# A Strassen-style down projection: weight sums made ahead of time in the attention, deeper look-ahead, and a later last statistic

## The chip, the cores and the metric

The kernel runs on one NeuronCore of a Trainium2 chip. A core has five engines that run their own instruction streams and meet at semaphores: TensorE (PE in the profile; PEld are its weight loads), VectorE (DVE), ScalarE (ACT), GpSimd (POOL) and SyncE (SP), which in this kernel only issues DMA transfers, all of them, from one queue, in order. The metric is device time in microseconds, the median of several runs.

## The reference, cut to what matters

One decoder layer on 1024 tokens of width 1024, in float32, with three sub-layers, each normalised before and after and added to the residual stream:

```python
for l in range(DEPTH):
    h = rmsnorm(x, g_mix_pre[l])
    ...                                    # S5 state space + chunked gMLP mixers
    x = x + rmsnorm(mix, g_mix_post[l])
    h = rmsnorm(x, g_x_pre[l])
    mem_n = rmsnorm(mem, g_mem[l])
    xa = memory_cross_attention(h, mem_n, w_q[l], w_k[l], w_v[l], w_o[l])   # 4 heads, 256 memory tokens
    x = x + rmsnorm(xa, g_x_post[l])
    h = rmsnorm(x, g_ffn_pre[l])
    f = conv_ffn(h, w_up[l], conv_w[l], conv_b[l], w_down[l])
    x = x + rmsnorm(f, g_ffn_post[l])

def conv_ffn(h, w_up, conv_w, conv_b, w_down):
    a = causal_depthwise_conv(h @ w_up, conv_w, conv_b)
    val, gate = jnp.split(a, 2, axis=-1)
    return (val * jax.nn.gelu(gate)) @ w_down        # w_down: 2816 x 1024
```

## The kernel before, in words

**Layout.** Activations are held transposed, channels on the 128 partitions and tokens along the free dimension, in tiles of 128x512, so each tensor has two token halves, h = 0 and 1. Every float32 matmul is made of three passes: an operand is split into a rounded part (an ACT cast) and a rest (a DVE or POOL subtraction), and high x high, high x low and low x high are summed in PSUM (`mm3`, the matmuls of L232). The splits of streamed weights are L130 and L133, those of other operands L251 and L252 (`split`).

**Stages.** `mixers`, `attention`, `ffn` and `down` follow each other in one program. A scheduler places the instructions of all stages on the engines by its own simulated times; each engine then runs its list strictly in order. Only where `self.pinned` is set does `pin` keep the written order. Tiles come from pools with a fixed number of buffers per tag ("b" 32, "m" 16, "w" 13, "raw" 4 and so on), and a transfer into a tile waits on SP until the buffer is free.

**Attention.** For each token half h, `attention` makes the queries of four heads (`q_block`), the scores and the softmax (`scores`), the transposes (`turn`), the weighted values (`weigh`) and the output projection (`proj`, "o2"). Beside it run generators: `post[h]` finishes the mixers' sub-layer (normalise at L722 on DVE, add the residual at L723 on POOL, sum the squares at L709), and `post2[h]` does the same for the attention. The q blocks of a half need `post[h]` to be done.

**Down projection.** `w_down` and the gated activations (kept in DRAM as `fd`) are taken as 2x2 blocks with 11 slices of 128 channels in each half of the contraction. Seven block products replace eight, after Strassen and Winograd:

- phase 0: W11·a and W12·b
- phase 1: S2·T2 and S1·T1
- phase 2: S3·T3 and S4·d
- phase 3: W22·T4

with S1 = W21 + W22, S2 = S1 − W11, S3 = W11 − W21, S4 = W12 − S2 on the weights, and T1 = c − a, T2 = d − T1, T3 = d − c, T4 = b − T2 on the activations, slice by slice. A phase has 11 steps k. In phases 0 to 2 a step is 24 matmuls of 128x512, 12 into the four "acc" banks (A) and 12 into three "sx" banks and the "st" bank (B), so three matmuls into `st` end each step. `d_prep(n)` walks ahead of PE: `d_load` issues a step's transfers, `d_sums` makes the sums (L1374; all on POOL but T1, which is on DVE), `d_split` makes four splits per step (L251 on ACT, L252 on DVE). Loads run 2 steps ahead of the splits, sums 1 step. At the ends of phases the banks are copied or added out (`ready`, L1445 to L1454).

**Tail.** Phase 3 is done by token quarters of 256. While the first quarter of token half 1 is multiplied, `first_half` squares and sums the finished half 0 (adds on DVE), and `finish` scales it (L765) and adds the residual `rs` loaded from DRAM (L766), both on DVE; there are 4 `rs` buffers for 8 residual tiles. Then the order is pinned; in the pass over the second quarter, the statistics of the first quarter are taken at `TAIL_R` (`rms`: matmuls at L277, then 11 small DVE instructions, L280 and L260 to L269) and broadcast at `TAIL_B` (`bcast`, L304), where a pair (b, k) names the block and the slice after which they stand.

Of the kernel before, what the change touches and what calls it, by code (L numbers as in the profile page):

```python
# [43 lines left out]
Q_STATS = 3  # L44
TAIL_R = (0, 7)
TAIL_B = (1, 4)
T_FROM = 11
T_RATE = 1
FETCH = 2
D_LOAD = 2  # L50
D_FIRST = {"S3": 1, "22": 2}
# [99 lines left out]
class Builder:  # L151
# [602 lines left out]
    def finish(self, m, acc, h, x2d):  # L754
# [8 lines left out]
        for i in range(KT):  # L763
            x = m[i]
            v.scalar_tensor_tensor(x, x, self.gain["g_ffn_post"][:, i:i + 1], bc, ALU.mult, ALU.mult)  # L765
            v.tensor_tensor(x, x, res[i], ALU.add)  # L766
            yield
            nc.sync.dma_start(self.out[P * i:P * i + P, HALF * h:HALF * h + HALF], x)
# [33 lines left out]
    def prepare(self, cp, dp):  # L802
# [71 lines left out]
        self.x2d = halves("x2d", 8)  # L874
        self.fd = halves("fd", NP)
        self.p1d = [dram(f"p1d{i}", [P, HALF]) for i in range(NP)]
        self.v0d = [dram(f"v0d{i}", [P, HALF]) for i in range(NP)]
# [168 lines left out]
    def attention(self):  # L1046
# [109 lines left out]
        sq2 = [None, None]  # L1156
        self.post2 = [None, None]
        for h in range(2):
            heads = lambda k, hh: oT[hh][k]
            for i in range(6):  # L1160
                if i == 5:
                    for b in range(EARLY):
                        begin(heads, "o2", b, h, range(6))
                if i == 1:
                    self.drain(post[h])
                if 1 <= i <= 4:
                    scores(h, i - 1)
                for j in range(2):
                    if i < 4:
                        q_block(h, i, j)  # L1170
                    if i >= 2:
                        turn(i - 2) if j == 0 else weigh(h, i - 2)
# [160 lines left out]


    def d_load(self, n):
        nc = self.nc
# [9 lines left out]
        if ph == 0:  # L1346
            get("11", w(0, 0), "b")
            get("12", w(0, 1), "raw")
            get("a", x(0, 1), "t" if n < 2 else "f")
            get("b", x(1, 1), "t" if n < 2 else "fr")  # L1350
        elif ph == 1:
            if k < 2:
                get("a", x(0, 1), "f")
            get("21", w(1, 0), "f")
            get("22", w(1, 1), "b")
            get("c", x(0, 0), "f")
            get("d", x(1, 0), "f")
        elif ph == 2:
            get("11", w(0, 0), "b")
            get("21", w(1, 0), "f")  # L1360
            get("12", w(0, 1), "raw")
            get("c", x(0, 0), "f")
# [5 lines left out]
    def d_sums(self, n):  # L1368
        v, g = self.nc.vector, self.nc.gpsimd
        ph, k = divmod(n, 11)  # L1370
        s = self.ds[k]

        def sub(key, to, x, y, e=g, op=ALU.subtract):
            e.tensor_tensor(s[to], s[x], s[y], op)  # L1374
            s[key] = s[to]

        if ph == 1:
            sub("S1", "22", "21", "22", g, ALU.add)
            sub("S2", "11", "S1", "11")
            sub("T1", "c", "c", "a", v)  # L1380
            sub("T2", "a", "d", "T1")
        elif ph == 2:
            sub("S3", "21", "11", "21")
            sub("S4", "S2", "12", "S2")
            sub("T3", "c", "d", "c")
# [3 lines left out]
    def d_split(self, n):  # L1389
# [3 lines left out]
        for i, key in enumerate(names):  # L1393
# [4 lines left out]
            hl = self.dp[n, i] = self.pair(tag)  # L1398
            self.split(*hl, s.pop(key) if key not in ("S2", "T2", "11", "a", "d") else s[key])

    def d_prep(self, n):

        while self.n_prep < min(n, 44):
            i = self.n_prep
            while self.n_load <= min(i + D_LOAD, self.d_last):
                self.d_load(self.n_load)
                self.n_load += 1
            while self.n_sums <= min(i + 1, 43):
                self.d_sums(self.n_sums)
                self.n_sums += 1  # L1410
# [9 lines left out]
    def down(self):  # L1420
# [54 lines left out]
        def first_half():  # L1475
            for b in range(8):
                self.sumsq(m[b], sq[0], b == 0, v)
                if b % 2:
                    yield
# [25 lines left out]
        self.drain(job)  # L1505
        self.pinned = True
        st = {}
        for b in range(4):
            for k in range(11):
                one(k, b, quarters[1])  # L1510
# [91 lines left out]
```

## Time and profile before

| | us |
|---|---|
| median of 3 runs | 1379.97 (1378.66 to 1382.13) |
| the profiled execution, whole | 1384.13 |
| its span, first to last instruction | 1382.4 |

In that execution the mean granted TensorE clock was 0.958. Times inside the trace count from the span's start. "Busy" of an engine leaves out waiting; "idle before, releaser" in a row is the time that the engine stood still just before those instructions, and what it waited for. Matmuls are pipelined, so the mean of one matmul record (some 390 ns) is longer than the spacing of two. In a row of windows the columns are the stretch, its length, the busy time of PE, PEld, DVE, ACT and POOL (with the number of instructions), the granted clock, the share of the DMA engines, and GB/s. The down projection begins near 1113 us; its phase 3 begins at 1319.75 us.

### The profile page before, as it was taken

To read this page: it belongs to the slowest core of one execution; us is meant where nothing else is said; L and a number is where in the kernel's file an instruction comes from. 1 tells how busy PE (TensorE), PEld (TensorE's weight loads), DVE (VectorE), ACT (ScalarE), POOL (GpSimd) and SP (SyncE) were. 2 spreads that over 40 slices of the span, in tenths; PEclk is the share of its full clock that TensorE was granted. 3 is DMA by queue.
4 is the path that set the end of the run, shared out by engine and by line. 5 is a ranking of instruction groups with operands and counts; after the bars stand their busy time and mean duration, and the time that the engine had idled before them with its cause. 6 is when DMAs were issued, how large, how long until landed. Compare 5 with 4: busy or idle time off the path is not lost. (4 is left out here: it accounts for less than half of the span.)

```text
span 1382.4 us, 19079 instructions
## 1 busy us (share of the span) xinstructions
PE 1281.1 (93%) x6352; PEld 1084.1 (78%) x6352; DVE 1064.7 (77%) x1645; ACT 627.3 (45%) x1172; POOL 662.5 (48%) x506
## 2 busy tenths in 40 slices
PE   9799998779998999989999999999999999896984
PEld 8689897678886887778887788888888887775883
DVE  7968799875375647785578969789988889997675
ACT  7223331246453545445445645555555553336340
POOL 1576346734254005420455477665664128995302
PEclk9899999889998999999999999999999999998996
DMA  9644326356344214452376674545554297556224
GB/s 314 191 140 133 89 82 174 84 154 182 99 123 152 64 53 142 134 157 62 114 244 208 210 257 156 165 146 162 165 156 145 77 336 243 178 171 214 77 70 152
DMA packets 139572, 213.38 MB, mean 154 GB/s; under 512 B 32464, under 2 KB 41808, under 8 KB 139472
## 3 DMA queue, kind: packets, MB, share of 16 engines
q1 hardware_dynamic: 139472, 212.15, 49.0%
q8 instruction: 50, 0.82, 0.2%
q14 instruction: 50, 0.41, 0.1%
HBM read 165.58 MB, written 42.32 MB: 150 GB/s over the span
## 5 line engine op out<-in xcount | busy, mean ns | idle before, releaser
L232 PE MATMUL acc<-b,w 128*128 128x512 f32 x2412 | 593.9, 399 | 26.1 <-ACT m L1450 11.0
L232 PEld LDWEIGHTS acc<-b,w 128*128 128x128 f32 x2412 | 461.2, 193 | 126.9 <-ACT m L1450 11.4
L133 DVE TENSOR_TENSOR w<-raw,w 128x512 fp32r<-128x512 f32 x206 | 194.3, 950 | 102.1 <-PE acc L232 72.8
L232 PE MATMUL sx<-b,w 128*128 128x512 f32 x921 | 223.7, 392 | 2.0 <-ACT T L1270 1.9
L232 PEld LDWEIGHTS sx<-b,w 128*128 128x128 f32 x921 | 174.3, 190 | 39.5 <-ACT T L1270 2.3
L130 ACT CAST w<-raw 128x512 fp32r<-128x512 f32 x228 | 141.4, 622 | 121.6 <-PE acc L232 69.7
L709 POOL TENSOR_TENSOR ac<-ac,sq 128x512 f32<-128x512 f32 x45 | 68.8, 1538 | 184.7 <-ACT sq L708 141.5
L232 PE MATMUL acc<-T,w 128*128 128x512 f32 x528 | 127.0, 389 | 0.0
L232 PEld LDWEIGHTS acc<-T,w 128*128 128x128 f32 x528 | 99.1, 188 | 20.5
L723 POOL TENSOR_TENSOR m<-m,rs 128x512 f32<-128x512 f32 x32 | 48.9, 1534 | 64.4 <-DVE m L722 30.2
L252 DVE TENSOR_TENSOR b<-f,b 128x512 fp32r<-128x512 f32 x53 | 66.8, 1267 | 10.8 <-ACT b L251 10.5
L232 PE MATMUL sx<-T,w 128*128 128x512 f32 x264 | 66.5, 389 | 0.0
L252 DVE TENSOR_TENSOR w<-b,w 128x512 fp32r<-128x512 f32 x44 | 57.3, 1305 | 6.6 <-PE acc L232 4.3
L251 ACT CAST b<-f 128x512 fp32r<-128x512 f32 x53 | 32.3, 619 | 64.0 <-DVE w L252 45.1
L232 PEld LDWEIGHTS sx<-T,w 128*128 128x128 f32 x264 | 49.6, 188 | 10.3
L708 ACT ACTIVATE sq<-m 128x512 f32<-128x512 f32 x66 | 41.4, 631 | 33.5 <-POOL m L723 14.2
L1209 POOL TENSOR_TENSOR b<-b,m 128x512 f32<-128x512 f32 x22 | 31.5, 1430 | 47.4 <-ACT m L1208 47.2
L114 POOL TENSOR_TENSOR st<-st,b 128x512 f32<-128x512 f32 x20 | 26.8, 1340 | 52.8 <-DMA st<-in_w_up 35.8
L232 PE MATMUL acc<-w,b 128*128 128x256 f32 x384 | 51.1, 291 | 0.0
L133 POOL TENSOR_TENSOR w<-raw,w 128x512 fp32r<-128x512 f32 x22 | 30.3, 1380 | 40.5 <-ACT w L130 25.4
L232 PEld LDWEIGHTS acc<-w,b 128*128 128x128 f32 x384 | 48.6, 197 | 0.1
L1374 POOL TENSOR_TENSOR f<-f,f 128x512 f32<-128x512 f32 x22 | 36.0, 1637 | 17.2 <-DMA f<-fd 12.4
(351 smaller groups left out, 2306.7 us busy)
## 6 DMA issues: line engine op xcount, KB each, us to landing
raw<-in_w_up SPq DMA_DIRECT2D x68, 256.0 KB, 2.9
f<-fd SPq DMA_DIRECT2D x55, 256.0 KB, 4.0
b<-in_w_up SPq DMA_DIRECT2D x40, 256.0 KB, 2.7
raw<-in_w_dk SPq DMA_DIRECT2D x33, 256.0 KB, 3.4
b<-in_w_dk SPq DMA_DIRECT2D x33, 256.0 KB, 3.7
raw<-in_w_out SPq DMA_DIRECT2D x32, 256.0 KB, 2.7
raw<-in_w_q SPq DMA_DIRECT2D x32, 256.0 KB, 2.7
raw<-in_w_o SPq DMA_DIRECT2D x32, 256.0 KB, 2.6
```

Source lines behind the costliest of these rows:

```text
L114: g.tensor_tensor(p["S4"], p["12"], p["S2"], ALU.subtract)
L130: nc.scalar.copy(hi[:, :w], t[:, :w])
L133: e.tensor_tensor(lo[:, :w], t[:, :w], hi[:, :w], ALU.subtract)
L232: self.pin(nc.tensor.matmul(ps, lhsT=x, rhs=y, start=first and i + j == 0, stop=last and i == n - 1 and j == 2, skip_group_check=go_on))
L251: self.nc.scalar.copy(hi, src)
L252: (e or self.nc.vector).tensor_tensor(lo, src, hi, ALU.subtract)
L708: nc.scalar.activation(sq, src, AF.Square)
L709: (e or nc.gpsimd).tensor_tensor(acc, acc, sq, ALU.add)
L723: g.tensor_tensor(x, x, rs, ALU.add)
L1209: nc.gpsimd.tensor_tensor(val, val, gate, ALU.mult)
L1374: e.tensor_tensor(s[to], s[x], s[y], op)
```

## The change

It has five parts.

1. A generator `s_sums` makes S1 to S4 of all 11 slices during the attention: for each slice four loads of `w_down` into "m" tiles, four POOL instructions, four stores to new DRAM tensors `sd`. It is advanced at fixed points of the head loop, 14 times per token half.
2. `d_load` fetches S1 to S4 from `sd` in phases 1 and 2 in place of the weight blocks (two weight tiles per step; before, two in phase 1 and three in phase 2), and `d_sums` keeps only T1 to T4, all on POOL, T1 too.
3. Loads run 4 steps ahead (`D_LOAD`), input sums 2 (`D_SUMS`).
4. In `first_half` the adds of the squares move from DVE to POOL, and in `finish` the residual add moves from DVE to POOL.
5. `TAIL_R` moves from (0, 7) to (1, 1), `TAIL_B` from (1, 4) to (1, 9), and the order is pinned from block 1 on, not from block 0.

```diff
-TAIL_R = (0, 7)
-TAIL_B = (1, 4)
+TAIL_R = (1, 1)
+TAIL_B = (1, 9)
-D_LOAD = 2
+D_LOAD = 4
+D_SUMS = 2
@@ finish
             v.scalar_tensor_tensor(x, x, self.gain["g_ffn_post"][:, i:i + 1], bc, ALU.mult, ALU.mult)
-            v.tensor_tensor(x, x, res[i], ALU.add)
+            g.tensor_tensor(x, x, res[i], ALU.add)
@@ attention
+        s_job = self.s_sums()
         for h in range(2):
             for i in range(6):
+                if i > 1:
+                    next(s_job, None)
...
                 for j in range(2):
+                    if i:
+                        next(s_job, None)
@@ new
+    def s_sums(self):
+        nc, g = self.nc, self.nc.gpsimd
+        for k in range(11):
+            t = {}
+            for o in range(2):
+                for j in range(2):
+                    t[o, j] = self.slot("m")
+                    nc.sync.dma_start(t[o, j], self.a["w_dk"][k + 11 * j][:, HALF * o:HALF * o + HALF])
+            yield
+
+            def put(n, to, x, y, op=ALU.subtract):
+                g.tensor_tensor(t[to], t[x], t[y], op)
+                nc.sync.dma_start(self.sd[n][k], t[to])
+
+            put(1, (1, 1), (1, 0), (1, 1), ALU.add)
+            put(3, (1, 0), (0, 0), (1, 0))
+            put(2, (0, 0), (1, 1), (0, 0))
+            put(4, (0, 1), (0, 1), (0, 0))
+            yield
@@ d_load
-            get("12", w(0, 1), "raw")
+            get("12", w(0, 1), "raw" if n < 2 else "b")
...
-            get("21", w(1, 0), "f")
-            get("22", w(1, 1), "b")
+            get("S2", self.sd[2][k], "b")
+            get("S1", self.sd[1][k], "b")
...
-            get("11", w(0, 0), "b")
-            get("21", w(1, 0), "f")
-            get("12", w(0, 1), "raw")
+            get("S3", self.sd[3][k], "b")
+            get("S4", self.sd[4][k], "b")
@@ d_sums
         if ph == 1:
-            sub("S1", "22", "21", "22", g, ALU.add)
-            sub("S2", "11", "S1", "11")
-            sub("T1", "c", "c", "a", v)
+            sub("T1", "c", "c", "a")
             sub("T2", "a", "d", "T1")
         elif ph == 2:
-            sub("S3", "21", "11", "21")
-            sub("S4", "S2", "12", "S2")
             sub("T3", "c", "d", "c")
@@ d_prep
-            while self.n_sums <= min(i + 1, 43):
+            while self.n_sums <= min(i + D_SUMS, self.d_last):
@@ down
-                self.sumsq(m[b], sq[0], b == 0, v)
-                if b % 2:
+                self.sumsq(m[b], sq[0], b == 0)
+                if b % 4 == 3:
                     yield
...
-        self.pinned = True
         st = {}
         for b in range(4):
+            self.pinned = b > 0
```

**How the order moves, place 1: POOL in the down projection, about steps 15 to 18.** Before, the sums of weights (into `b`) stand between those of activations (into `f`).

```order
L1374 TENSOR_TENSOR b1851_10878<-b1990_11436,b1851_10878 128x512
L1374 TENSOR_TENSOR f1889_11026<-f2030_11603,f2029_11601 128x512
L1374 TENSOR_TENSOR b2002_11489<-f2001_11487,b2002_11489 128x512
L1374 TENSOR_TENSOR b1843_10862<-raw2104_11919,b1843_10862 128x512
L1374 TENSOR_TENSOR f1901_11074<-f2043_11658,f2042_11656 128x512
L709 TENSOR_TENSOR ac1842_10861<-ac1842_10861,sq2013_11539 128x512
```

Now, at the same adds of squares (`ac`):

```order
L1400 TENSOR_TENSOR f1929_11214<-f2069_11776,f2068_11774 128x512
L1400 TENSOR_TENSOR f2081_11827<-f2081_11827,f1941_11262 128x512
L1400 TENSOR_TENSOR f1941_11262<-f2082_11829,f2081_11827 128x512
L1400 TENSOR_TENSOR f2094_11880<-f2094_11880,f1953_11310 128x512
L1400 TENSOR_TENSOR f1953_11310<-f2095_11882,f2094_11880 128x512
L710 TENSOR_TENSOR ac1886_11081<-ac1886_11081,sq2065_11767 128x512
```

Only sums of activations are left, and T1 (the rows whose first source is their own tile) has come over from DVE.

**Place 2: POOL in the attention, token half 1**, between the adds of squares at the end of `post[1]` and the residual adds of `post2[0]` (L723, now L724). `ac` are sums of squares, `rs` residuals, `m` both the outputs and the tiles of `s_sums`. Before:

```order
L709 TENSOR_TENSOR ac831_5223<-ac831_5223,sq891_5465 128x512
L709 TENSOR_TENSOR ac823_5177<-ac823_5177,sq896_5488 128x512
L709 TENSOR_TENSOR ac823_5177<-ac823_5177,sq904_5530 128x512
L709 TENSOR_TENSOR ac823_5177<-ac823_5177,sq912_5592 128x512
L723 TENSOR_TENSOR m822_5175<-m822_5175,rs936_5769 128x512
```

Now the last rows of that stretch, of 13 sums (L1354) in all before the same residual add:

```order
L710 TENSOR_TENSOR ac851_5333<-ac851_5333,sq940_5748 128x512
L1354 TENSOR_TENSOR m961_5907<-m961_5907,m960_5905 128x512
L1354 TENSOR_TENSOR m988_6030<-m986_6026,m988_6030 128x512
L1354 TENSOR_TENSOR m986_6026<-m989_6032,m986_6026 128x512
L1354 TENSOR_TENSOR m987_6028<-m987_6028,m986_6026 128x512
L1354 TENSOR_TENSOR m1011_6169<-m1010_6167,m1011_6169 128x512
L1354 TENSOR_TENSOR m1010_6167<-m1008_6163,m1010_6167 128x512
L1354 TENSOR_TENSOR m1008_6163<-m1011_6169,m1008_6163 128x512
L1354 TENSOR_TENSOR m1009_6165<-m1009_6165,m1008_6163 128x512
L1354 TENSOR_TENSOR m1031_6302<-m1030_6300,m1031_6302 128x512
L724 TENSOR_TENSOR m850_5331<-m850_5331,rs968_5933 128x512
```

In token half 0, the other 28 sums stand together, after the adds of `post[0]` and before those of `post[1]`, where POOL had nothing.

**Place 3: DVE in the tail.** Before, the last scalings of token half 0, the eight residual adds, then the statistic of the first quarter:

```order
L765 SCALAR_TENSOR_TENSOR m2135_12035<-m2135_12035,gains_84,st2332_12860 128x512
L766 TENSOR_TENSOR m2128_12000<-m2128_12000,rs2320_12788 128x512
L766 TENSOR_TENSOR m2129_12005<-m2129_12005,rs2321_12790 128x512
L766 TENSOR_TENSOR m2130_12010<-m2130_12010,rs2322_12792 128x512
L766 TENSOR_TENSOR m2131_12015<-m2131_12015,rs2323_12794 128x512
L766 TENSOR_TENSOR m2132_12020<-m2132_12020,rs2324_12796 128x512
L766 TENSOR_TENSOR m2133_12025<-m2133_12025,rs2325_12798 128x512
L766 TENSOR_TENSOR m2134_12030<-m2134_12030,rs2326_12800 128x512
L766 TENSOR_TENSOR m2135_12035<-m2135_12035,rs2327_12802 128x512
L280 TENSOR_SCALAR st_x_12985<-st_12982 128x2
```

Now:

```order
L766 SCALAR_TENSOR_TENSOR m2181_12226<-m2181_12226,gains_84,st2361_12982 128x512
L766 SCALAR_TENSOR_TENSOR m2182_12231<-m2182_12231,gains_84,st2361_12982 128x512
L766 SCALAR_TENSOR_TENSOR m2183_12236<-m2183_12236,gains_84,st2361_12982 128x512
L281 TENSOR_SCALAR st_x_13161<-st_13158 128x2
L261 TENSOR_SCALAR rs_y2_13163<-st_x_13161 128x2
```

All eight scalings (now L766) still stand ahead of the statistic; the eight residual adds (now L767) are on POOL, after seven adds of squares there and ahead of POOL's share of the first quarter (L774, L776).

More of the change, by code (lines that the diff above doesn't have):

```diff
@@ L875, in prepare @@
         self.fd = halves("fd", NP)
+        self.sd = {n: [dram(f"sd{n}_{i}", [P, HALF]) for i in range(11)] for n in range(1, 5)}
         self.p1d = [dram(f"p1d{i}", [P, HALF]) for i in range(NP)]
@@ L1368, in d_sums, with sub @@
     def d_sums(self, n):
-        v, g = self.nc.vector, self.nc.gpsimd
         ph, k = divmod(n, 11)
         s = self.ds[k]
-        def sub(key, to, x, y, e=g, op=ALU.subtract):
-            e.tensor_tensor(s[to], s[x], s[y], op)
+        def sub(key, to, x, y):
+            self.nc.gpsimd.tensor_tensor(s[to], s[x], s[y], ALU.subtract)
             s[key] = s[to]
         if ph == 1:
-            sub("S1", "22", "21", "22", g, ALU.add)
-            sub("S2", "11", "S1", "11")
-            sub("T1", "c", "c", "a", v)
+            sub("T1", "c", "c", "a")
             sub("T2", "a", "d", "T1")
         elif ph == 2:
-            sub("S3", "21", "11", "21")
-            sub("S4", "S2", "12", "S2")
             sub("T3", "c", "d", "c")
@@ L1398, in d_split @@
             hl = self.dp[n, i] = self.pair(tag)
-            self.split(*hl, s.pop(key) if key not in ("S2", "T2", "11", "a", "d") else s[key])
+            self.split(*hl, s.pop(key) if key not in ("T2", "a", "d") else s[key])
     def d_prep(self, n):
```

## The prediction

> **What bounds the kernel now.** I read the page first, then a table of stretches, then the places where PE stands still.
>
> ```profile
> span 1382.4 us, 19079 instructions
> PE 1281.1 (93%) x6352; PEld 1084.1 (78%) x6352; DVE 1064.7 (77%) x1645; ACT 627.3 (45%) x1172; POOL 662.5 (48%) x506
> 432.00:530.00 98.00, 97.89 (x491) 82.58 (x490) 49.07 (x110) 41.09 (x89) 2.08 (x2) 0.98 0.23 68
> 563.00:612.00 49.00, 44.72 (x223) 37.24 (x222) 40.52 (x80) 22.61 (x49) 19.05 (x13) 0.93 0.49 149
> 612.00:650.00 38.00, 37.56 (x201) 31.62 (x200) 21.87 (x53) 19.28 (x43) 0.62 (x1) 1.00 0.20 60
> 1113.00:1173.20 60.20, 60.20 (x266) 49.57 (x264) 52.30 (x58) 27.70 (x49) 33.82 (x21) 1.00 0.85 298
> 1173.20:1319.80 146.60, 127.81 (x530) 103.66 (x530) 123.03 (x109) 63.16 (x119) 101.07 (x62) 0.92 0.50 160
> 1319.80:1382.40 62.60, 38.04 (x297) 37.26 (x295) 40.16 (x86) 14.67 (x33) 8.90 (x6) 0.83 0.33 110
> ```
>
> PE is the bound nearly everywhere (93%). The rows are, in order, the heads of token half 0, those of half 1 (two rows), phase 0 of the down projection, its phases 1 and 2, and phase 3 with the tail. In phase 0 PE never stops. In phases 1 and 2 DVE and POOL are full and PE is not; in the tail nobody is.
>
> The time lost in phases 1 and 2 is read from the matmuls that end each step (into `st`):
>
> ```profile
> 1128.88 0.84 PE L232 MATMUL st<-b,w 128*128 128x512 f32 x3
> 1134.32 0.84 PE L232 MATMUL st<-b,w 128*128 128x512 f32 x3
> ...
> 1172.40 0.84 PE L232 MATMUL st<-b,w 128*128 128x512 f32 x3
> ...
> 1177.87 6.45 PE L232 MATMUL acc<-b,w 128*128 128x512 f32 x15 [4.63 <-ACT m L1445]
> ...
> 1257.50 6.17 PE L232 MATMUL acc<-b,w 128*128 128x512 f32 x16 [11.02 <-ACT m L1450]
> ...
> 1319.07 0.84 PE L232 MATMUL st<-b,w 128*128 128x512 f32 x3
> ```
>
> A step without a stall takes 1134.32 − 1128.88 = 5.44 us. From the end of step 10 (1172.40) to that of step 32 (1319.07) are 146.67 us for 22 steps, which need 119.68. So **27.0 us** are lost, with slow matmuls behind each stall (16 in 6.17 us). ACT is named, but ACT itself stands behind DVE (40.1 us in this stretch, casts that wait for a split's buffer), and DVE stands behind POOL:
>
> ```profile
> 1146.52 0.69 DVE L252 TENSOR_TENSOR b<-f,b 128x512 fp32r<-128x512 f32 x1
> 1148.31 1.74 POOL L1374 TENSOR_TENSOR b<-f,b 128x512 f32<-128x512 f32 x1
> 1148.82 1.78 DVE L252 TENSOR_TENSOR w<-b,w 128x512 fp32r<-128x512 f32 x1
> 1150.01 1.74 POOL L1374 TENSOR_TENSOR f<-f,f 128x512 f32<-128x512 f32 x1
> 1150.52 1.78 DVE L252 TENSOR_TENSOR b<-fr,b 128x512 fp32r<-128x512 f32 x1
> ...
> ACT b L251 <- DVE w L252: 40.1, 7, 10.0
> L1198 DVE SCALAR_TENSOR_TENSOR m<-acc,conv,m 128x511 f32<-128x511 f32 x44 | 32.7, 743 | 7.8 <-ACT m L1195 7.8
> L709 POOL TENSOR_TENSOR ac<-ac,sq 128x512 f32<-128x512 f32 x2 | 2.6, 1296 | 85.9 <-ACT sq L708 85.8
> ```
>
> Alone, a DVE split takes 0.69 us and a POOL add 1.30 (the last row, of 432 to 530 us, where POOL did only two). Together they take turns: one of each per 1.70 us, and the DVE instruction reads 1.78, so it loses 1.09. DVE instructions with a PSUM source keep their time beside a busy POOL (743 ns mean over 44). So each POOL instruction delays at most one DVE instruction with two SBUF sources, by 1.09 us.
>
> **The change part by part.** Weight sums out of the down projection:
>
> ```profile
> L1374 POOL TENSOR_TENSOR b<-f,b 128x512 f32<-128x512 f32 x11 | 19.0, 1738 | 0.0
> L1374 POOL TENSOR_TENSOR f<-b,f 128x512 f32<-128x512 f32 x11 | 17.7, 1605 | 15.2 <-DMA b<-in_w_dk 10.9 <-DMA f<-fd 3.6 <-DVE b L252 0.6
> L1374 DVE TENSOR_TENSOR f<-f,f 128x512 f32<-128x512 f32 x11 | 15.0, 1367 | 0.0
> ACT b L251 <- DMA f<-in_w_dk: 9.0, 1, 9.0
> ```
>
> Four such groups of 11 on POOL (S1 to S4) go, and the 11 T1 cross from DVE to POOL. Before, the 22 steps hold 62 POOL and 109 DVE instructions: 62 x 1.70 + 47 x 0.61 = 134 us, more than PE's 119.7, hence the stalls. After, POOL has at most 22 (T1, T2) + 11 (T3) + 11 (T4) + 3 adds of squares = 47, and DVE 98: 47 x 1.70 + 51 x 0.61 = 111 us, below 119.7; with some ten of the T1 and T2 made in phase 0 already, about 100. A step of phase 1 needs 2 x 1.70 + 2 x 0.61 = 4.6 of its 5.44 us. So PE is the bound again. I keep 2 us for the hand-over of the banks between phases: **−25 us**. Bounds: −27 if nothing is left; −14 if the 11.02 us stall stays and 2 more. It began with a late load (9.0 us, `f<-in_w_dk`); that load is gone, and loads go 4 steps ahead, which is why I stay near the first.
>
> Transfers are hidden: the down projection has fewer, and the attention gets 88 more of 256 KB. With 56 of them in 98 us, 68 GB/s become some 218; phase 0 ran at 298 with PE at 60.20 of 60.20.
>
> The sums in the attention are 44 POOL instructions:
>
> ```profile
> L133 DVE TENSOR_TENSOR w<-raw,w 128x512 fp32r<-128x512 f32 x25 | 18.3, 733 | 25.8 <-PE acc L232 18.8 <-issue 2.7 <-PE st L232 2.6
> L1122 DVE SCALAR_TENSOR_TENSOR mx<-mx,rs_y 128x2 f32<-128x2 f32 x8 | 1.2, 159 | 0.2
> ...
> 598.26 0.66 PE L1140 MATMUL sx<-ident,t 128*128 128x128 f32 x4 [1.68 <-ACT t L1126]
> 599.83 0.56 PE L232 MATMUL sx<-kv,t 128*128 128x256 f32 x2 [0.91 <-ACT t L251]
> 601.76 0.58 PE L232 MATMUL sx<-kv,t 128*128 128x256 f32 x1 [1.37 <-DVE t L252]
> ```
>
> Half 0: 28 x 1.74 = 49 us of POOL fit into 98 us in which it did 2.08. They delay at most 28 DVE instructions, 30.5 us, and DVE had 49 of 98. On PE only chains count that have no slack: the two `mx` products per head (L1122) sit between the scores and the transposes, 8 x 1.09 = 8.7 us at worst. I take 3. Half 1: 16 sums, 13 of them ahead of the residual adds of `post2[0]`, in a place where DVE has 40.5 of 49 us and PE already waits for the softmax (1.68 + 0.91 + 1.37). 40.5 + 16 x 1.09 = 58 does not fit into 49; over the 87 us to 650 it does (80). At worst 9 us come out on PE; I take 4. Together **+7** (0 to +18), near the lower end since both stretches have room on average. SP has more to do, but its loads here wait for buffers anyway:
>
> ```profile
> SPq L84 <- DVE w L133: 257.0, 103, 11.2
> raw<-in_w_dk SPq DMA_DIRECT2D x33, 256.0 KB, 3.4
> fd<-m SPq DMA_DIRECT2D x22, 256.0 KB, 2.2
> ```
>
> The tail:
>
> ```profile
> 1341.06 5.39 DVE L765 SCALAR_TENSOR_TENSOR m<-m,gains,st 128x512 f32<-128x512 f32 x8 [2.52 <-ACT st L307]
> 1346.36 2.49 DVE L766 TENSOR_TENSOR m<-m,rs 128x512 f32<-128x512 f32 x4
> 1352.67 0.69 DVE L766 TENSOR_TENSOR m<-m,rs 128x512 f32<-128x512 f32 x1 [1.84 <-DMA rs<-x2d]
> 1354.91 0.15 DVE L280 TENSOR_SCALAR st_x<-st 128x2 f32<-128x2 f32 x1
> 1357.18 1.20 PE L304 MATMUL st<-ident,rs_y 128*128 128x128 f32 x4 [12.46 <-DVE rs_y L269]
> ...
> 1358.37 11.42 PE acc L232 x84
> ```
>
> PE loses 12.46 us because the statistic stands on DVE behind eight scalings (5.39) and eight residual adds that wait for late loads. The adds go to POOL, so it looks as if some 8.5 us came free: scalings 5.4 plus small instructions 2.3 against 1357.18 − 1341.06 = 16.1. But POOL's adds follow each scaling at once, and both read two SBUF sources: DVE #1 and #2 run free (1.2 us), the other six one per 1.70 (10.2), two of the small ones meet POOL's last adds (3.4), nine run free (1.8): 16.6 us. The stall stays as long as it was; PE has 15 more matmuls before it and 15 fewer behind. **0 us**, bounds −8.5 (no turn-taking) and +3 (POOL's seven adds of squares come late: 7 x 1.74 = 12.2 where DVE had 0.69 each). The end after the last matmul is the same chain.
>
> [...]
>
> Sum: 1384.13 − 25 + 7 + 0 = 1366.1 for a run like the profiled one, which lies 4.16 above the median; so **1362 us**.
>
> **The rivals.**
>
> - *The attention gives most of it back.* For: DVE at 40.5 of 49 us, chains without slack. Against: POOL empty for 85.9 us. +18: 1380 − 25 + 18 = 1373.
> - *Everything comes free.* No turn-taking in the tail, slack in the attention: 1380 − 27 + 1 − 8.5 = 1346. For: POOL could be held back by late `rs` loads there; against: the first four are loaded long before.
> - *Loads bound phases 1 and 2.* SP is in order and four steps of look-ahead need buffers: −14 + 7, 1373. For: the 9.0 us wait; against: one weight tile less per step of phase 2.
> - *Slower: the 28 sums hold up `post[1]`.* They stand ahead of its residual adds on POOL, and the q blocks of half 1 wait for those. A slice alone takes load 3.4, sums 7.0, store 2.2, and on SP two weight loads in between that wait 257.0/103 = 2.5 each: 17.6 us. If slices go one after another, seven take 123 us from 432 on and end at 555, 25 us after the place where `post[1]` starts (530): 1380 − 25 + 25 + 7 = 1387. It decides from 14 us per slice on. Against: eight "m" buffers are free, two slices, so loads and sums overlap.
>
> **How the numbers follow.** Forecast 0.52 (its own range 1354 to 1371), attention 0.15, everything 0.14, loads 0.10, slower 0.09. A measurement of this kernel can tell about 0.3% (4.1 us) from no change. Faster: 0.52 + 0.14 + 0.09 + 0.07 = 0.82 (of the two at 1373, 0.09 and 0.07); within: 0.04 + 0.03 + 0.02 = 0.09; slower: 0.02 + 0.07 = 0.09. The range 1347 to 1378 leaves out half of "everything", and "slower".
>
> **What would show it.** Right: steps 11 to 32 at 5.44 us each, about 122 us together, DVE below full; a PE stall of 10 us or more on the second statistic, with L766 at 1.78 beside L767; PE losing 5 to 10 us more between 430 and 650. Wrong: stalls in phase 1 on transfers; a `post[1]` that starts after 545; a tail stall under 6 us.

## The result, and the profile after

The changed kernel takes 1373.56 us (median of 8 runs, 1370.69 to 1375.76) where the kernel before, run beside it, takes 1381.88 us (8 runs, 1378.66 to 1386.55). The ratio is 0.9936, with a 95% interval of 0.9917 to 0.9956. So the change gains 8.3 us, and the forecast said 18.

The page of the changed kernel, and a table of stretches cut at the same events as the prediction's (columns as there: length, PE, PEld, DVE, ACT, POOL, granted clock, DMA share, GB/s):

```profile
span 1373.8 us, 19246 instructions
PE 1275.9 (93%) x6352; PEld 1080.4 (79%) x6352; DVE 1066.1 (78%) x1619; ACT 628.0 (46%) x1172; POOL 694.6 (51%) x532
```

```profile
432.00:530.00 98.00, 97.77 (x490) 82.27 (x489) 59.44 (x110) 40.84 (x89) 41.14 (x30) 0.98 0.65 212
563.00:625.00 62.00, 47.43 (x216) 37.72 (x215) 53.20 (x79) 22.97 (x50) 41.50 (x29) 0.86 0.74 253
1125.30:1185.75 60.45, 60.45 (x267) 49.75 (x265) 57.95 (x53) 27.44 (x49) 45.23 (x26) 1.00 0.90 323
1185.75:1310.40 124.65, 121.61 (x531) 100.56 (x531) 87.49 (x105) 65.51 (x120) 35.79 (x23) 0.99 0.46 146
1310.40:1373.80 63.40, 38.61 (x296) 37.69 (x295) 43.57 (x71) 14.61 (x32) 32.49 (x21) 0.82 0.33 108
```

Phases 1 and 2 (the fourth stretch) are what the change was to relieve: 124.65 us where they took 146.60, DVE busy 87.49 us of it where it was 123.03, POOL 35.79 where it was 101.07, and the clock is back at 0.99. Half 0's heads (the first stretch) take 41 us of POOL and three times the bytes without any loss on PE (97.77 of 98.00 us). The loss is in the second stretch, the heads of half 1: PE is busy 47.43 of 62 us there, at a clock of 0.86 (before, 44.72 of 49 us at 0.93, up to the same event).

The steps of phases 1 and 2, by PE's timeline:

```profile
1179.47 0.84 PE L233 MATMUL st<-b,w 128*128 128x512 f32 x3
1184.91 0.84 PE L233 MATMUL st<-b,w 128*128 128x512 f32 x3
1188.80 5.07 PE L233 MATMUL acc<-b,w 128*128 128x512 f32 x14 [3.04 <-ACT m L1467]
...
1200.74 0.84 PE L233 MATMUL st<-b,w 128*128 128x512 f32 x3
...
1309.54 0.84 PE L233 MATMUL st<-b,w 128*128 128x512 f32 x3
```

Steps 11 to 32 take 1309.54 − 1184.91 = 124.6 us, 22.0 less than before. One stall of 3.04 us is left, at the hand-over of the banks to phase 1, where DVE is still full from phase 0 (57.95 of 60.45 us in the third stretch above). The two steps across it take 15.8 us (1184.91 to 1200.74) where two take 10.9; the other 20 take 5.44 us each on the mean.

Three differences make up the 8.6 us between the spans. Step 10 ends at 1184.91 where it ended at 1172.40: **+12.5**. Steps 11 to 32: **−22.0**. From there to the end 64.26 us instead of 63.33: **+0.9**.

The +12.5 arise in one place. Up to the second half nothing has moved (the statistic of half 0's o2 products is broadcast on PE at 528.10 before and at 528.25 after). Then, in PE's timeline of the changed kernel:

```profile
568.14 1.05 PE L278 MATMUL st<-ones,ac 128*128 128x1 f32 x8 [0.94 <-POOL ac L710]
576.85 0.95 PE L278 MATMUL st<-ones,ac 128*128 128x1 f32 x8
585.97 1.11 PE L233 MATMUL sx<-kv,t 128*128 128x256 f32 x4 [3.47 <-ACT t L252]
591.22 1.13 PE L305 MATMUL st<-ident,rs_y 128*128 128x128 f32 x8 [0.18 <-DVE rs_y L270]
611.40 1.12 PE L1142 MATMUL sx<-ident,t 128*128 128x128 f32 x4 [7.15 <-ACT t L1128]
```

and in that of the kernel before:

```profile
567.06 0.95 PE L277 MATMUL st<-ones,ac 128*128 128x1 f32 x8
572.18 0.96 PE L277 MATMUL st<-ones,ac 128*128 128x1 f32 x8
582.14 1.05 PE L304 MATMUL st<-ident,rs_y 128*128 128x128 f32 x8
```

The first statistic (of `post[1]`, from which the scores' scale is made) is 1.1 us later on PE, the second (of `post2[0]`) 4.7, its broadcast 9.1, and the second transposes of the heads 611.40 − 598.26 = 13.1, with PE standing still for 3.47 us ahead of the second head's scores (ACT's cast of its queries, L252, stands behind the first head's softmax) and for 7.15 ahead of the transposes. DVE shows what happens between. The root of the first statistic in the changed kernel, and the first products that wait for it:

```profile
573.95 0.15 DVE L281 TENSOR_SCALAR st_x<-st 128x4 f32<-128x4 f32 x1
574.13 1.07 DVE L261 TENSOR_SCALAR rs_y<-st_x 128x4 int32<-128x4 int32 x1
575.24 1.21 DVE L263 TENSOR_TENSOR rs_t<-rs_y 128x4 f32<-128x4 f32 x1
576.48 1.19 DVE L269 SCALAR_TENSOR_TENSOR rs_t<-rs_t,st_x 128x4 f32<-128x4 f32 x1
577.71 1.21 DVE L270 SCALAR_TENSOR_TENSOR rs_y<-rs_t,rs_y 128x4 f32<-128x4 f32 x1
...
582.09 0.17 DVE L739 TENSOR_SCALAR rs_y<-rs_y 128x4 f32<-128x4 f32 x1
582.17 0.68 DVE L1123 TENSOR_REDUCE mx<-sx 128x2 f32<-128x512 f32 x1
```

Eleven instructions on 128x4 numbers, each waiting for the one before it; six of them read 1.07 to 1.21 us instead of 0.16. The chain takes 8.2 us; before, it ran from 571.82 to 574.65, 2.8 us, with a weight split in it. POOL at the same time:

```profile
570.51 1.28 POOL L710 TENSOR_TENSOR ac<-ac,sq 128x512 f32<-128x512 f32 x1
571.76 1.72 POOL L1354 TENSOR_TENSOR m<-m,m 128x512 f32<-128x512 f32 x1
573.70 1.48 POOL L1354 TENSOR_TENSOR m<-m,m 128x512 f32<-128x512 f32 x1 [0.23 <-issue]
575.14 1.29 POOL L710 TENSOR_TENSOR ac<-ac,sq 128x512 f32<-128x512 f32 x1
576.39 5.26 POOL L1354 TENSOR_TENSOR m<-m,m 128x512 f32<-128x512 f32 x4
```

Two things can be read here. The additions of the new sums (L1354) run beside the small instructions and stretch them. And they stand between the last additions of squares (L710), so that the second statistic has its sum later.

### The profile page after: what moved, and what is told of

The parts are those of the page before. It is cut to its first block, busy times and chain, and to the rows that moved or that the text cites. A ratio compares the mean times of both kernels' runs of the same rounds, so it can differ in the third digit from the quotient of the medians.

```text
span 1373.8 us, 19246 instructions
## 1 busy us (share of the span) xinstructions
PE 1275.9 (93%) x6352; PEld 1080.4 (79%) x6352; DVE 1066.1 (78%) x1619; ACT 628.0 (46%) x1172; POOL 694.6 (51%) x532
## 5 line engine op out<-in xcount | busy, mean ns | idle before, releaser
L233 PE MATMUL acc<-b,w 128*128 128x512 f32 x2412 | 587.9, 397 | 11.4 <-DVE b L730 4.4
L134 DVE TENSOR_TENSOR w<-raw,w 128x512 fp32r<-128x512 f32 x206 | 203.1, 994 | 94.2 <-PE acc L233 64.6
L710 POOL TENSOR_TENSOR ac<-ac,sq 128x512 f32<-128x512 f32 x52 | 78.3, 1513 | 153.2 <-ACT sq L709 152.6
L253 DVE TENSOR_TENSOR w<-b,w 128x512 fp32r<-128x512 f32 x64 | 67.4, 1065 | 23.7 <-PE st L233 8.6
L1400 POOL TENSOR_TENSOR f<-f,f 128x512 f32<-128x512 f32 x33 | 55.0, 1678 | 48.1 <-DMA f<-fd 35.5
L1354 POOL TENSOR_TENSOR m<-m,m 128x512 f32<-128x512 f32 x44 | 62.8, 1432 | 31.3 <-DMA m<-in_w_dk 22.3
L724 POOL TENSOR_TENSOR m<-m,rs 128x512 f32<-128x512 f32 x32 | 49.3, 1545 | 48.6 <-DMA rs<-x1d 18.9
L253 DVE TENSOR_TENSOR b<-f,b 128x512 fp32r<-128x512 f32 x53 | 54.4, 1041 | 4.3 <-ACT b L252 4.0
L252 ACT CAST w<-b 128x512 fp32r<-128x512 f32 x64 | 39.5, 619 | 27.3 <-PE acc L233 16.9
L252 ACT CAST b<-f 128x512 fp32r<-128x512 f32 x53 | 32.7, 619 | 38.4 <-DVE w L253 34.3
```

The source lines that it names most:

```text
L134: e.tensor_tensor(lo[:, :w], t[:, :w], hi[:, :w], ALU.subtract)
L233: self.pin(nc.tensor.matmul(ps, lhsT=x, rhs=y, start=first and i + j == 0, stop=last and i == n - 1 and j == 2, skip_group_check=go_on))
L252: self.nc.scalar.copy(hi, src)
L253: (e or self.nc.vector).tensor_tensor(lo, src, hi, ALU.subtract)
L710: (e or nc.gpsimd).tensor_tensor(acc, acc, sq, ALU.add)
L724: g.tensor_tensor(x, x, rs, ALU.add)
```

## The experiments

Three theories for the loss in half 1. **A**: the additions stretch DVE's instructions, the small ones of the statistics above all. **B**: the additions stand ahead of other POOL work in its order. **C**: their transfers delay weights and residuals. All runs, with the ratio to the kernel before that ran beside them (the changed kernel did not run beside the others, so a difference from it is safer by the ratios than by the medians):

| run | us | ratio, 95% interval |
|---|---|---|
| the changed kernel | 1373.56 | 0.9936 [0.9917, 0.9956] |
| sums alone | 1392.34 | 1.0100 [1.0076, 1.0125] |
| no additions in half 1 | 1360.46 | 0.9853 [0.9827, 0.9879] |
| slices issued later | 1373.48 | 0.9951 [0.9936, 0.9966] |
| additions held late | 1364.05 | 0.9870 [0.9853, 0.9886] |
| roots through PSUM | 1369.14 | 0.9919 [0.9893, 0.9944] |
| half 1's additions on DVE | 1370.80 | 0.9917 [0.9900, 0.9935] |
| short look-ahead | 1374.54 | 0.9949 [0.9928, 0.9971] |
| tail undone | 1372.35 | 0.9934 [0.9919, 0.9949] |
| scalings from PSUM in the tail | 1368.07 | 0.9903 [0.9883, 0.9922] |
| statistic first in the tail | 1368.39 | 0.9915 [0.9889, 0.9941] |
| combination | 1344.96 | 0.9750 [0.9718, 0.9782] |
| combination, statistic first | 1346.82 | 0.9763 [0.9729, 0.9797] |
| combination, early additions | 1351.05 | 0.9765 [0.9742, 0.9788] |

### Sums alone

The kernel before with `s_sums`, its DRAM tiles and the calls in `attention`; `d_load` and `d_sums` stay as they were.

```diff
+        s_job = self.s_sums()
...
+                if i > 1:
+                    next(s_job, None)
...
+                    if i:
+                        next(s_job, None)
```

> The kernel before, with the 44 weight sums of the attention added and stored and nothing else changed: nobody reads what they store, and the down projection makes its own sums as before. If the changed kernel's 12.5 us of delay at step 10 of the down projection come from the sums in the attention, this is 11 to 14 us slower than the kernel before (1381.88 us): about 1394, ratio 1.009. If the sums are hidden and the delay comes from what stands in the FFN or at the start of the down projection (loads four steps ahead), it is within 3 us of the kernel before, 1382 to 1385.

Measured: 1.0100 times the kernel before, 11.9 us slower by the medians. The attention alone costs what the trace put there (in this run's trace the last broadcast of `post2[1]` comes at 707.53, 11.1 us after that of the kernel before), and the rest of the change is worth the difference of the two ratios, (1.0100 − 0.9936) x 1381.88 = 22.7 us.

### Additions left out, transfers kept

```diff
-                g.tensor_tensor(t[to], t[x], t[y], op)
+                if k < 7:
+                    g.tensor_tensor(t[to], t[x], t[y], op)
```

> The changed kernel; for the last four of the 11 slices, those of token half 1 of the attention, the 16 additions on POOL are left out (what was loaded is stored as it is, so four slices of the sums are wrong), while all loads and stores stay. Theory A (turns with POOL make the small DVE instructions of the statistics long): no POOL instruction runs beside them, the transposes come about 11 us earlier, 1361 to 1365. Theory B (additions stand ahead of other POOL work in its queue): the same. Theory C (the transfers of these slices delay weights and residuals): nothing changes, 1371 to 1375.

Measured: 1360.46 us, 13 less than the changed kernel. Every load and store of the four slices is still there (299 and 357 GB/s between 550 and 600 us), and the second transposes come at 596.35, as early as in the kernel before (598.26). The root's instructions are back at 0.16 us each. Theory C is refuted; the cost is in POOL's 16 additions.

### The same slices, issued later

```diff
-                if i > 1:
+                if i > (1, 2)[h]:
...
-                    if i:
+                    if i > (0, 2)[h]:
```

> The changed kernel with the last four slices issued from head group 3 of token half 1 on, where they began at group 1: the statistics of post[1] and post2[0] then run ahead of them. Theories A and B: the 12.5 us shrink to 2 to 5, so 1364 to 1368, unless the later additions lie beside the o2 projection's squares and cost there what they cost before. Theory C: the same bytes in less time, 1372 to 1380.

Measured: no difference from the changed kernel, but the run didn't do what it was to do. In POOL's timeline the first addition of half 1 is still ahead of the squares:

```profile
568.15 1.54 POOL L1354 TENSOR_TENSOR m<-m,m 128x512 f32<-128x512 f32 x1 [1.68 <-DMA rs<-x1d]
569.65 2.52 POOL L710 TENSOR_TENSOR ac<-ac,sq 128x512 f32<-128x512 f32 x2
```

The scheduler fills POOL by its own simulated times, and the additions went where POOL looked free. It decides between no theories. The next run fixes the order.

### Additions held behind the residual additions

```diff
-            g.tensor_tensor(x, x, rs, ALU.add)
+            ins = g.tensor_tensor(x, x, rs, ALU.add)
+            if mode == "f" and h == 0:
+                self.tc.keep_in_program_order(ins)
...
+                if k > 6:
+                    self.tc.keep_in_program_order(ins)
...
             self.xg[h] = []
+            if h:
+                self.drain(s_job)
```

where in the loop of half 1 `next(s_job)` is called only once the eight residual additions are emitted.

> The changed kernel with the 16 additions of the last four slices kept, in POOL's order, behind the eight residual additions of post2[0] (both held in program order), and their loads and stores emitted after the last step of half 1's loop, ahead of the second o2 projection. The shift that the run before this one failed to make. Theory A (turns: the statistics' small DVE instructions stretched) and theory B (additions ahead of other POOL work): both give back the 12.5 us less what 16 additions of 1.3 to 1.7 us cost beside the o2 projection: 1361 to 1367. If it stays at 1371 to 1376, the additions cost the same wherever they lie in half 1, and neither place nor queue is the cause.

Measured: 1364.05 us, 9.5 less than the changed kernel, and the intervals are apart. POOL now:

```profile
603.34 2.62 POOL L724 TENSOR_TENSOR m<-m,rs 128x512 f32<-128x512 f32 x2 [4.11 <-DMA rs<-x1d]
605.91 12.19 POOL L1361 TENSOR_TENSOR m<-m,m 128x512 f32<-128x512 f32 x8
622.07 5.93 POOL L1361 TENSOR_TENSOR m<-m,m 128x512 f32<-128x512 f32 x4 [3.97 <-DMA m<-in_w_dk]
630.57 5.84 POOL L1361 TENSOR_TENSOR m<-m,m 128x512 f32<-128x512 f32 x4 [2.56 <-DMA raw<-in_w_o]
```

The second transposes come at 597.52. The same 16 additions, 28 to 41 us later, cost 3.6 us by the medians (1360.46 without them) instead of 13.1, and 2.3 instead of 11.5 by the ratios. SP issues the first eight of their loads between 556 and 569 us in both kernels, so it is the place of the additions that costs. A and B both say this; the next run asks for A.

### Roots through PSUM

The prediction had read that DVE instructions with a PSUM source keep their time beside POOL (743 ns, mean of 44). So the root's estimate `y` is kept in the statistic's PSUM bank, and each instruction then has at most one input in SBUF.

```diff
+        self.pin(v.tensor_scalar(y.bitcast(I32), xp.bitcast(I32), -0.5, 1597463007.0, ALU.mult, ALU.add))
+        for n in range(3):
+            self.pin(v.scalar_tensor_tensor(t, y, -0.5, x, ALU.mult, ALU.mult))
+            self.pin(v.tensor_tensor(t, y, t, ALU.mult))
+            self.pin(v.scalar_tensor_tensor(r if n == 2 else y, t, 1.5, y, ALU.add, ALU.mult))
```

> The changed kernel; the reciprocal square root of each statistic keeps one operand of every DVE instruction in PSUM (one instruction more per statistic), since DVE instructions with a PSUM source were not lengthened beside POOL in the trace. Theory A: the chain for the score scale of half 1, 8.2 us from 573.95 to 582.17 in the changed kernel, comes to about 3, that of post2[0], 5.5 us, to about 3; transposes 6 to 8 us earlier, 1365 to 1368. Theory B: the chain is not what is late, 1372 to 1375. Theory C: 1372 to 1375.

The chain of the first statistic in this run, POOL beside it, and PE at the first statistic and at the second transposes:

```profile
577.14 0.15 DVE L281 TENSOR_SCALAR st_x<-st 128x4 f32<-128x4 f32 x1
...
579.18 0.16 DVE L295 SCALAR_TENSOR_TENSOR rs_y<-rs_t,st 128x4 f32<-128x4 f32 x1
579.38 0.27 DVE L753 TENSOR_SCALAR rs_y<-rs_y 128x4 f32<-128x4 f32 x1
...
574.94 3.43 POOL L1368 TENSOR_TENSOR m<-m,m 128x512 f32<-128x512 f32 x2
578.33 1.29 POOL L724 TENSOR_TENSOR ac<-ac,sq 128x512 f32<-128x512 f32 x1
...
571.32 1.05 PE L278 MATMUL st<-ones,ac 128*128 128x1 f32 x8 [1.58 <-POOL ac L724]
607.70 1.12 PE L1156 MATMUL sx<-ident,t 128*128 128x128 f32 x4 [6.03 <-ACT t L1142]
```

2.5 us instead of 8.2. The time is 1369.14 us, 4.4 less than the changed kernel by the medians and 2.3 by the ratios; the intervals overlap, so the times leave the size open. In this trace the first statistic is already 3.2 us later than in the changed kernel (571.32 for 568.14), so I compare the way from there to the second transposes: 31.2 us before, 43.3 in the changed kernel, 36.4 here. By the traces 6.9 of the 12.1 us go with the stretched roots, as A has it, and 5.2 are another part.

### The additions of half 1 on DVE

```diff
-                g.tensor_tensor(t[to], t[x], t[y], op)
+                (g if k < 7 else nc.vector).tensor_tensor(t[to], t[x], t[y], op)
```

> The changed kernel with the 16 additions of the last four slices on DVE instead of POOL. Theory A: nothing is stretched (a DVE addition takes 0.69 us alone, the statistics' chains 2.6 us each), but the 16 additions stand in DVE's order, 11 us of work, and each may hold DVE up until its load lands: 1364 to 1370. Theory B: POOL's queue is clear, 1361 to 1365. If the added DVE work itself is what costs, 1372 or more.

Measured: 1370.80 us, 0.8 above A's range. The additions are cheaper (0.81 us mean), but DVE stands still for their operands:

```profile
L1354 DVE TENSOR_TENSOR m<-m,m 128x512 f32<-128x512 f32 x16 | 12.9, 807 | 12.1 <-DMA rs<-x1d 7.7 <-DMA m<-in_w_dk 4.3
```

12.9 us of work and 12.1 us of waiting in the engine that everything else in half 1 needs. Moving the work off POOL did not help for a reason of its own, so this run does not tell A from B.

### The tail

The tail took as long as before, as the prediction had worked out. The rows of the changed kernel:

```profile
1333.33 11.47 DVE L766 SCALAR_TENSOR_TENSOR m<-m,gains,st 128x512 f32<-128x512 f32 x8 [1.38 <-ACT st L308]
1334.15 12.98 POOL L767 TENSOR_TENSOR m<-m,rs 128x512 f32<-128x512 f32 x8 [9.62 <-DVE m L766]
1344.72 0.15 DVE L281 TENSOR_SCALAR st_x<-st 128x2 f32<-128x2 f32 x1
1348.86 1.19 PE L305 MATMUL st<-ident,rs_y 128*128 128x128 f32 x4 [11.94 <-DVE rs_y L270]
```

The eight scalings take 11.47 us beside POOL's additions, where scalings and additions together took 13.9 on DVE, waits for loads included. PE waits 11.94 us for the second statistic (12.46 before).

First, the tail's edits undone:

```diff
-TAIL_R = (1, 1)
-TAIL_B = (1, 9)
+TAIL_R = (0, 7)
+TAIL_B = (1, 4)
...
-            g.tensor_tensor(x, x, res[i], ALU.add)
+            v.tensor_tensor(x, x, res[i], ALU.add)
...
-                self.sumsq(m[b], sq[0], b == 0)
+                self.sumsq(m[b], sq[0], b == 0, v)
```

> The changed kernel with its last two parts undone: first_half's squares are added on DVE and finish's residual additions are on DVE again, and the last statistics are emitted where they were. The turn-taking of the prediction: DVE has 5.4 + 5.5 us for scalings and additions instead of 11.5 for scalings beside POOL, the same; no change, 1371 to 1376. If moving the additions was a real relief that only the trace's last matmul hides: 1378 to 1382.

Measured: 0.9934 against the changed kernel's 0.9936. These edits are worth nothing, and the traces agree: from the end of step 32 to the end are 64.24 us here and 64.26 in the changed kernel. Second, the scalings read the broadcast where it lies, in PSUM:

```diff
-        return r, self.bcast(r, nt)[1]
+        return r, self.bcast(r, nt)[ps]
...
-        r, bc = yield from self.stats(acc, 4)
+        r, bc = yield from self.stats(acc, 4, 0)
```

(the second pair of lines in `finish` alone; `ps` is 1 elsewhere).

> The changed kernel; finish's eight scalings (L766) read the broadcast from its PSUM bank where they read a copy in SBUF. If DVE's turns with POOL are taken only by instructions whose operands all lie in SBUF, the eight take about 5.9 us where they took 11.47 beside POOL's additions, the stall of 11.94 us on the second statistic falls to 6 or 7, and the time is 5 to 6 us lower: 1367 to 1369. If the PSUM operand doesn't matter, 1372 to 1375.

DVE, POOL and PE of that run:

```profile
1328.87 5.36 DVE L766 SCALAR_TENSOR_TENSOR m<-m,gains,st 128x512 f32<-128x512 f32 x8 [1.39 <-ACT st L308]
1329.69 6.17 POOL L767 TENSOR_TENSOR m<-m,rs 128x512 f32<-128x512 f32 x5 [9.74 <-DVE m L766]
1334.37 0.99 PE L278 MATMUL st<-ones,ac 128*128 128x1 f32 x4 [6.16 <-DVE m L766]
```

The same eight scalings take 5.36 us, with POOL's additions running at 1.23 us each beside them, and the stall halves: PE now waits 6.16 us for the `st` bank, which the scalings hold. From the end of step 32 to the end are 57.72 us instead of 64.26. The time is 5.5 us lower by the medians, as the first reading expected, and 4.6 by the ratios, whose intervals just overlap. So what made the tail's edit worthless is the turn-taking, and these scalings take turns only with both large operands in SBUF: 11.47 us for the eight, 5.36 with one of the two in PSUM. Third, the statistic ahead of the scalings in DVE's order:

```diff
+                    self.pinned = True
                     st["r"] = self.rms(sq[1][:, quarters[0]], 2)
+                    self.drain(job)
```

with `TAIL_R = (0, 3)`, `finish` stopped behind its broadcast until then, and its scalings pinned.

> The changed kernel; in the tail the statistic of the first token quarter is held, in DVE's order, ahead of finish's eight scalings (L766), which are held behind it. If the place in DVE's order makes the stall of 11.94 us, it falls below 2 us, and what ends the tail is then DVE's own sequence of scalings, squares and products: 1363 to 1369. If DVE's total work bounds the tail either way, the stall moves to the last square and the time stays at 1371 to 1375.

```profile
1333.36 11.61 DVE L767 SCALAR_TENSOR_TENSOR m<-m,gains,st 128x512 f32<-128x512 f32 x8
1355.40 1.02 PE L278 MATMUL st<-ones,ac 128*128 128x1 f32 x4 [9.20 <-DVE ac L1517]
```

The stall on the second statistic is gone (PE runs from 1330.67 to 1346 without one), and 9.20 us stand in front of the last statistic instead, for which DVE's last square came late. By the trace both expectations are half right: 58.81 us from the end of step 32 to the end, and 1368.39 us, 5.2 less by the medians and 2.9 by the ratios (the intervals overlap).

### Look-ahead

```diff
-D_LOAD = 4
-D_SUMS = 2
+D_LOAD = 2
+D_SUMS = 1
```

> The changed kernel with the look-ahead of before: loads two steps ahead and input sums one (part 3 of the change undone, the sums still read from DRAM). If the 22 us of phases 1 and 2 come from DVE's lighter order alone, 1372 to 1376. If loads two steps ahead come late now that four 256 KB tiles a step are wanted, or POOL's sums hold the splits up, the steps grow by 0.2 to 0.5 us each: 1378 to 1385.

Measured: 0.9949 against 0.9936, no difference that can be told, and steps 11 to 32 take 124.8 us in its trace (1181.12 to 1305.91) as in the changed kernel. So the 22 us of phases 1 and 2 come from part 2 of the change: the weight sums no longer made there, T1 on POOL, and one weight tile less to load per step of phase 2. No run separates these three.

### The versions that follow from it

Late additions, roots through PSUM, and the scalings ahead of the residual additions (in `post`, `post2` and `finish`) reading the broadcast in PSUM; the second scaling of `post2`, by `g_ffn_pre`, still reads SBUF. Beside the edits shown, in `post`:

```diff
-        r, bc = yield from self.stats(acc, 4)
+        r, bc = yield from self.stats(acc, 4, 0)
         yield
         acc2 = self.slot("ac")
```

> The late additions of the earlier run (1364.05 us), with the statistics' roots through PSUM and with all scalings of post, post2 and finish reading the broadcast from its PSUM bank. From the parts: 5.5 us for the tail, up to 2 us for the eight scalings of post2[0], up to 1 us for the roots, since no addition runs beside them any more: 1355 to 1359. If holding the one st bank longer delays the next statistic or the early o2 products, 1360 to 1366.

Measured: 1344.96 us, 0.975 [0.9718, 0.9782], 36 us faster than the kernel before and 28.6 faster than the change (25.7 by the ratios). That is 10 us below the expected range, mostly because the scalings' time was on the path in places that the expectation put at nothing. The group of all 32 scalings of `post` and `post2`, in the changed kernel (first row) and here:

```profile
L723 DVE SCALAR_TENSOR_TENSOR m<-m,gains,st 128x512 f32<-128x512 f32 x32 | 39.4, 1295 | 4.5 <-ACT st L308 4.5
```

```profile
L737 DVE SCALAR_TENSOR_TENSOR m<-m,gains,st 128x512 f32<-128x512 f32 x32 | 21.5, 742 | 4.8 <-ACT st L322 4.7
```

Against the run with late additions alone, PE is 3.7 us earlier at the broadcast of half 0's o2 statistic (524.53 for 528.25), 6.9 at the second transposes of half 1 (590.60 for 597.52), 11.6 at the broadcast of the last o2 statistic (690.05 for 701.68), and 15.45 at step 10 of the down projection (1159.85 for 1175.30); the tail behind step 32 gives another 6.4 (56.74 us for 63.14). The roots alone do not give the first of these: the run that changed only them has 529.95 there. The kernel before had 1295 ns per scaling too: this part has nothing to do with the change.

The same with the statistic first in the tail (that run's edit, and in `finish` the broadcast's copy in SBUF again):

> As the combination, but in the tail the statistic of the first quarter ahead of the scalings (those read the SBUF copy again, since the bank is wanted by the statistic). If the order in DVE is worth more than the PSUM operand: 1352 to 1357; if less, 1358 to 1363.

Measured: 1346.82 us, below both expectations as the combination itself was, and the same as the combination within the intervals. The times do not tell the two remedies of the tail apart (behind step 32 the traces have 59.21 us here and 56.74 there), and they exclude each other, since `finish` holds the only `st` bank while it reads the broadcast there.

And the combination without the edit that holds the additions late, so that those of half 1 are where the change has them:

> The combination (1344.96 us, ratio 0.975), but with the last four slices' additions where the change put them, ahead of post2[0]'s squares and residual additions. The statistics' roots and all scalings have a PSUM operand, so DVE's turns no longer stretch them; what is left of the early additions' cost is the queue on POOL. Theory A, stretched DVE instructions cost the 12 us: within 3 us of the combination, 1344 to 1348, ratio 0.975 to 0.977. Theory B, POOL's queue: the 9.5 us between the changed kernel and the run with late additions remain, 1352 to 1357, ratio 0.980 to 0.983.

Measured: 1351.05 us, 0.9765 [0.9742, 0.9788], by the ratio inside A's expectation, by the time between the two. With roots and scalings reading PSUM (0.16 us for an instruction of a root in the run with the roots alone, 742 ns for a scaling in the combination), the early place costs 2 us by the ratios and 6 by the medians; the intervals overlap. In the trace PE's second statistic comes at 573.67 where the combination has 568.27. Of these 5.4 us, 4.0 are there at the first statistic already (563.78 for 559.75), 1.3 of them since half 0 (525.81 for 524.53); the rest comes because on POOL

```profile
567.38 3.44 POOL L1368 TENSOR_TENSOR m<-m,m 128x512 f32<-128x512 f32 x2
570.79 1.28 POOL L724 TENSOR_TENSOR ac<-ac,sq 128x512 f32<-128x512 f32 x1
```

the last addition of squares (L724 in this kernel) stands behind two of the new sums. So A and B both hold, and A is the larger part. From the first statistic to the second transposes the change adds 12.1 us (43.3 for 31.2), unstretched roots take away 6.9 of them, and with roots and scalings reading PSUM the early place adds 2.3 (33.2 for the combination's 30.9). These are single traces, and the intervals of the times overlap, so exact shares are not settled.

## Why the prediction was right or wrong

**Phases 1 and 2, −25: right, 22.0 measured.** The steps run at 5.44 us, DVE is below full, and the stall of 11 us went with its late load. For the 2 us kept for the hand-over of the banks, 4.9 came: 3.04 as a stall, the rest as slow matmuls behind it (14 in 5.07 us). I had worked out that DVE would be relieved inside phases 1 and 2, and had counted some ten of T1 and T2 as made in phase 0, but not asked what that does to DVE there: it is full (57.95 of 60.45 us) when the first bank is handed over.

**The attention, +7: the step that failed.** It was made of 3 for half 0 and 4 for half 1. Half 0 cost 0.15 us, and by the last broadcast of `post2[1]` (709.09 for 696.44) it is 12.65, so half 1 took 12.5: the 4 us for half 1 is the term that failed. The working for half 1 compared DVE's load with its room (58 us into 49, 80 into 87), and the only chains without slack that were priced were the two `mx` products per head, in half 0. It missed the chains that are there: two statistics of 11 or 12 small instructions each, one behind the other on DVE, for which the score scale and then the scalings wait. The price per meeting was about right (1.09 us; the small ones lost 0.91 to 1.05); what was wrong was which instructions would meet POOL. The prediction had even counted "two of the small ones" for the same chain in the tail, and the trace of the kernel before has one such meeting: L260 takes 0.92 us at 430.53, while POOL adds squares until 432.8. And "13 of them ahead of the residual adds" was named and not followed: ahead of them on POOL also stand the squares, and the second statistic waits for the last of those. The bound of 18 held.

**The tail, 0: right** in time and in reason: 11.47 us for the scalings (10.2 + 1.2 predicted), 15.5 from the first scaling to the broadcast (16.6 predicted), a stall of 11.94 us. Undoing the edits changes nothing, and taking the turns away by a PSUM operand shortens the tail by 6.5 us in the trace.

**The rivals.** "The attention gives most of it back" lies at the measured time, but with the wrong sum: it has +18 and −25 where 12.5 and −22.0 came. "Loads bound phases 1 and 2" has the same 1373 and is refuted by the steps of 5.44 us and by the run with the short look-ahead. "The 28 sums hold up `post[1]`" did not happen: the additions of half 0's seven slices end at 492.8, and `post[1]` starts at 528. "Everything comes free" is refuted by half 1.

**By the sums:** −22.0 + 12.5 + 0.9 = −8.6 in the profiled executions, where −25 + 7 + 0 = −18 was predicted: 5.5 us of the error from the attention, 3.0 from the down projection, 0.9 from the tail.

## What to carry to other kernels

When work is moved to an engine that has room, list the serial chains of small instructions that will run beside it, and price each instruction of such a chain, not the mean room: here a root of a dozen instructions of 0.16 us grew by 5 us, while 28 additions beside the heads of half 0, from 434.5 to 492.8 us, where only the last instruction of a root still ran (434.66, 1.16 us), cost 0.15 us. Room on average says little about a place where an in-order engine has a statistic's input behind the new work; hold the new work behind it, and look at the order that comes out, since the code's place alone moved nothing. And where DVE and POOL must work side by side, an operand that lies in PSUM anyway is worth reading there (here 742 ns a scaling for 1295), if its bank can be held that long: in the tail PE then waited 6.16 us for it.

## What the runs showed of the hardware

How far one PSUM operand goes was unexpected. A product of three inputs with 128x512 in SBUF, 128x512 in PSUM and a column of gains takes 742 ns (mean of 32, L737 in the combination) where POOL works beside it, and 1295 with the second one in SBUF (L723 in the changed kernel); alone, with both in SBUF, it takes 748 (mean of eight, L765 in the tail of the kernel before, where POOL stood still). In the tail POOL's additions fall from 1.62 us (12.98 for eight) to 1.23 (6.17 for five) beside them. The rows of the first statistic in the changed kernel also show when a stretched instruction ends: L261 at 575.20 and L263 at 576.45, POOL's additions beside them, which began first, at 575.18 and 576.43. So these two ended 0.02 us after the addition beside them, and lost 0.91 and 1.05 us of its 1.48 and 1.29.

One SBUF source alone did not keep an instruction's time. L261 has a single one and was stretched as well (1.07 us in half 1, 1.04 in the tail; 0.17 in the tail of the kernel before, where POOL stood still), as were two that scale the softmax, a tile by a column of sums, in the run with the roots through PSUM (2.57 us for the two, 0.62 for the next two). So the prediction's count of DVE instructions with two SBUF sources left some out; no run here separates what made these wait.
